# Wide products as halves outside attention, operands 64 bytes aside, and weight forms in another order

## The chip, the cores and the metric

The kernel runs on one core of a Trainium2 chip. The metric is the device time of one execution in microseconds, the median of several runs; lower is better. On the core TensorE multiplies (PE in the profile; its weight loads are PEld), VectorE (DVE) and ScalarE (ACT) work elementwise, GpSimd (POOL) and SyncE (SP) mostly issue DMAs. Each engine runs its own instructions in a fixed order and waits on semaphores for the others.

## The reference

A trunk of two decoder layers on 512 tokens of width 1024, in float32. Layer 0 mixes tokens by attention (8 forgetting heads, 8 stick-breaking heads), layer 1 by a gated short convolution. After each comes an MLP with a causal convolution of width 3 between up-projection and gate, inner width 2816. What the change touches is this (`rms_norm` and `causal_dwconv`, the sum of three shifted products, left out):

```python
def short_conv_mixer(h, norm_g, w_in, conv_w, w_out):
    xn = rms_norm(h, norm_g)
    proj = xn @ w_in
    gate_b = proj[..., :CONV_WIDTH]
    gate_c = proj[..., CONV_WIDTH:2 * CONV_WIDTH]
    u = proj[..., 2 * CONV_WIDTH:]
    y = gate_b * causal_dwconv(gate_c * u, conv_w)
    return y @ w_out

def conv_ffn(h, norm_g, w_up, conv_w, w_down):
    xn = rms_norm(h, norm_g)
    u = causal_dwconv(xn @ w_up, conv_w)
    g, val = u[..., :D_FF], u[..., D_FF:]
    return (jax.nn.silu(g) * val) @ w_down
```

The result of each mixer and of each MLP is added to the running activations.

## The kernel before

**Arithmetic.** A float32 operand is split into a high part, rounded to TensorE's reduced format (fp32r), and the low part that is left. A product is three matmuls: high by high, low by high, high by low. Of a weight block ScalarE makes the high part `whi` and VectorE, from it, the low part `wlo`. Both stand in rings of three buffers, so a form can be made only when TensorE has done with the third one before it.

**Two kinds of product.** A plain product (`mm3`) is three matmuls of 128 rows by 512 tokens. It is used in attention, in its output projection, in the first two of the eleven groups of columns of the first MLP, in the first block of the convolution's input projection and in its output projection. The others are made by a scheme of seven products for a 2 by 2 block multiplication (class `Sevens`): each group of 256 columns has seven weight forms, sums of quarter blocks X, Y, W, Z, and seven forms of the activations, named p1, p7, p3, p6, p2, q5, q4. Each of the seven is 24 matmuls of 256 tokens (line 1083). Quarter blocks come by DMAs issued by SP, and by accumulating DMAs issued by POOL. `Sevens.slot(g, s)` emits product number s of group g and behind it what later ones need: `weights_of` makes a weight form (lines 1031 and 1033), `kept` copies a bank of results (P7s and Xs) out before it is written again, `left`, `early` and `join` bring finished quarters to SBUF. In slot 4 `Xs` is copied from the bank to which q5 then adds. `table` is set for the two MLPs and not for the convolution. The convolution's forms carry a c in their names (`whi_q5c3` is form q5 of group 3); an MLP's carry layer and group (`wlo_p202` is form p2, layer 0, group 2).

**Down projections.** Line 1685, also by seven forms. In layer 0 the weights' 256 columns stream past activations as weights of the array; in layer 1 it is the other way, and 512 columns stream: 462 such matmuls. The activations' forms for it (`act`) take the places of the forms p6 and p2 of the up projection, their weights `whi` and `wlo` come by `load` (lines 317 and 318).

**Stages**, by the trace: attention to 256.7 us, its output projection's end to 273.5, plain blocks of the first MLP to 319.3, its seven-form blocks to 491, its down projection to 602, the convolution's first block to 626, its seven-form blocks to 727, its output projection to 772, the second MLP's up projection to 990, its down projection to 1103.

**What sets the order.** A scheduler takes the emitted program and orders each engine's instructions by modelled times and priorities; `pin` keeps an instruction at its place in the program, and `behind(x, y)` puts x after y. `spend(us)` tells it how much time of TensorE has passed, and `chores` (elementwise work left over, such as the convolution taps at line 449 and the scaling at lines 1343 and 1351) are worked off at a given rate. So an edit in one place can move instructions elsewhere. In the last MLP's start (L74 in the profile) the order is strictly that of the program.

## Time and profile before

| | us |
|---|---|
| median of 3 runs | 1109.64 (1108.37 to 1110.54) |
| the profiled execution | 1110.35 |
| its span, first to last instruction | 1108.2 |
| TensorE busy | 1089.2 |
| VectorE busy | 960.3 |
| ScalarE busy | 683.7 |
| POOL busy | 181.3 |

The granted clock of TensorE was 1.000 throughout. A row of the timeline has start and duration in microseconds, engine, line, operation, output and inputs, shapes, and in brackets the idle time before it and what ended it. Numbers of names are left out there. Matmuls overlap in the record: a row of 0.28 us may have its successor start 0.11 later, and it is the starts that tell the pace. A row of the waits names the engine, what waited, for what, and then the total in us, how many times, and the longest.

### The profile page before, as it was taken

How to read it: one execution, taken by the hardware profiler on the slowest of the kernel's cores; microseconds unless marked ns; L12 is line 12 of the kernel's file. 1: busy time of each engine (PE TensorE's matmuls, PEld its weight loads, DVE VectorE, ACT ScalarE, POOL GpSimd, SP SyncE). 2: the span in 40 equal slices, each digit the busy share in tenths (PEclk: the TensorE clock that was granted, in tenths of full speed). 3: DMA queues.
4: the chain of work that ended last, by engine and by line, in shares of the span. 5: the costliest groups of instructions: out<-in, count | busy, mean ns of one | idle time of the engine just before them, and what ended most of it. 6: DMA issues, size and time to landing. Idle time of an engine off the chain costs nothing.

```text
span 1108.2 us, 19897 instructions
## 1 busy us (share of the span) xinstructions
PE 1089.2 (98%) x7875; PEld 992.0 (90%) x7875; DVE 960.3 (87%) x1482; ACT 683.7 (62%) x1020; POOL 181.3 (16%) x206
## 2 busy tenths in 40 slices
PE   9999999999999999999999999999999999999998
PEld 7888787878889999999998899877999999998886
DVE  6798898997899788799979889776899999899886
ACT  7466667655567667676558655545666657567653
POOL 4011111101012221014401001011111221014300
PEclk9999999999999999999999999999999999999999
DMA  6678878688578988899955766596979887799951
GB/s 197 171 182 197 204 172 220 177 220 228 157 178 206 202 207 196 216 274 217 230 164 142 179 153 154 118 259 173 218 184 217 200 208 182 206 273 201 244 147 57
DMA packets 178109, 214.10 MB, mean 193 GB/s; under 512 B 7676, under 2 KB 143916, under 8 KB 178016
## 3 DMA queue, kind: packets, MB, share of 16 engines
q0 software_dynamic: 53280, 95.34, 44.6%
q1 hardware_dynamic: 124576, 117.42, 33.2%
q8 instruction: 62, 1.02, 0.3%
q14 instruction: 31, 0.25, 0.1%
q10 hardware_dynamic: 160, 0.07, 0.0%
HBM read 205.72 MB, written 44.04 MB: 225 GB/s over the span
## 4 chain that ended last, share of the span: by engine, by line
PE 57%; issue 14%; DVE 14%; DMA 9%; ACT 3%; POOL 1%; SPq 1%; DVEq 0%; ACTq 0%; POOLq 0%
PE psb L1685 10%; PE psb L1083 8%; PE psa L1685 7%; DMA three<-in_ffn_w_up 5%; PE psb L338 5%; PE psb L340 4%; PE psb L339 4%; PE psa L1083 3%; DVE wlo_p L1033 3%; PE psb L714 2%; DMA raw<-in_conv_w_out 2%; PE psa L811 2%; DMA Xc<-in_conv_w_in 1%; DMA raw<-in_ffn_w_down 1%; DVE wlo L318 1%
## 5 line engine op out<-in xcount | busy, mean ns | idle before, releaser
L1083 PE MATMUL psb<-p_hi,whi_p 128*128 128x256 f32 x480 | 132.9, 277 | 0.0
L1083 PE MATMUL psb<-p_hi,wlo_p 128*128 128x256 f32 x480 | 132.5, 276 | 0.1
L1083 PE MATMUL psb<-p_lo,whi_p 128*128 128x256 f32 x480 | 132.6, 276 | 0.0
L317 ACT ACTIVATE whi<-raw 128x1024 fp32r<-128x1024 f32 (+2 forms) x77 | 79.0, 1027 | 74.8 <-PE psb L339 22.0
L318 DVE TENSOR_TENSOR wlo<-raw,whi 128x1024 fp32r<-128x1024 f32 (+2 forms) x77 | 90.9, 1181 | 26.7 <-ACT whi L317 26.2
L1083 PE MATMUL psb<-q_hi,wlo_q 128*128 128x256 f32 x320 | 89.3, 280 | 2.0 <-DVE wlo_q L1033 1.9
L1083 PE MATMUL psa<-p_hi,wlo_p 128*128 128x256 f32 x320 | 89.9, 281 | 1.2 <-DVE wlo_p L1033 0.8
L1083 PEld LDWEIGHTS psb<-p_hi,wlo_p 128*128 128x128 f32 x480 | 90.0, 188 | 0.4 <-DVE wlo_p L74 0.4
L1083 PEld LDWEIGHTS psb<-p_hi,whi_p 128*128 128x128 f32 x480 | 90.1, 188 | 0.0
L1083 PEld LDWEIGHTS psb<-p_lo,whi_p 128*128 128x128 f32 x480 | 90.1, 188 | 0.0
L1083 PE MATMUL psb<-q_hi,whi_q 128*128 128x256 f32 x320 | 88.7, 277 | 0.3 <-ACT Xs L1145 0.2
L1083 PE MATMUL psa<-p_lo,whi_p 128*128 128x256 f32 x320 | 88.6, 277 | 0.0
L1083 PE MATMUL psa<-p_hi,whi_p 128*128 128x256 f32 x320 | 88.6, 277 | 0.0
L1083 PE MATMUL psb<-q_lo,whi_q 128*128 128x256 f32 x320 | 88.4, 276 | 0.0
L338 PE MATMUL psb<-hs_a,whi 128*128 128x512 f32 x176 | 72.9, 416 | 0.0
L340 PE MATMUL psb<-hs_a,wlo 128*128 128x512 f32 x176 | 69.6, 396 | 0.0
L1083 PEld LDWEIGHTS psa<-p_hi,wlo_p 128*128 128x128 f32 x320 | 60.0, 188 | 3.2 <-DVE wlo_p L1033 2.6
L1083 PEld LDWEIGHTS psb<-q_hi,wlo_q 128*128 128x128 f32 x320 | 60.0, 188 | 3.2 <-DVE wlo_q L1033 2.8
L1685 PE MATMUL psb<-act,whi 128*128 128x256 f32 x352 | 60.8, 277 | 0.9 <-DVE act L1035 0.7
L1083 PEld LDWEIGHTS psb<-q_hi,whi_q 128*128 128x128 f32 x320 | 60.1, 188 | 0.7 <-ACT Xs L1145 0.4
L1083 PEld LDWEIGHTS psa<-p_hi,whi_p 128*128 128x128 f32 x320 | 60.1, 188 | 0.3 <-ACT whi_p L1031 0.2
L1083 PEld LDWEIGHTS psa<-p_lo,whi_p 128*128 128x128 f32 x320 | 60.1, 188 | 0.0
(554 smaller groups left out, 3647.0 us busy)
## 6 DMA issues: line engine op xcount, KB each, us to landing
t<-in_ffn_w_up POOLq DMA_DIRECT2D x24, 768.0 KB, 8.2
raw<-in_attn_w_in SPq DMA_DIRECT2D x24, 512.0 KB, 5.2
t<-in_ffn_w_up POOLq DMA_DIRECT2D x12, 1024.0 KB, 10.3
X<-in_ffn_w_up SPq DMA_DIRECT2D x20, 512.0 KB, 5.0
Y<-t SPq DMA_DIRECT2D x20, 512.0 KB, 7.3
three<-t SPq DMA_DIRECT2D x20, 512.0 KB, 5.7
W<-in_ffn_w_up SPq DMA_DIRECT2D x20, 512.0 KB, 3.8
Z<-in_ffn_w_up SPq DMA_DIRECT2D x20, 512.0 KB, 5.6
```

The costliest lines, as they stand in the source:

```text
L317: return (act.activation(hi[:, at_], raw[:, at_], AF.Copy), dve.tensor_tensor(lo[:, at_], raw[:, at_], f32(hi[:, at_]), op=ALU.subtract))
L318: dve.tensor_tensor(lo[:, at_], raw[:, at_], f32(hi[:, at_]), op=ALU.subtract))
L338: made = [pe.matmul(acc, w[0], rhs[0], start=first, stop=False), pe.matmul(acc, w[0], rhs[1], start=False, stop=False), pe.matmul(acc, w[1 ...
L339: pe.matmul(acc, w[0], rhs[1], start=False, stop=False),
L340: pe.matmul(acc, w[1], rhs[0], start=False, stop=last)]
L714: pe.matmul(ss[e][:, c:c + wide], ql[rows, b * P:n], kl[rows, 0:wide], start=first and b == bs[0], stop=last and b == bs[-1])
L811: pe.matmul(out_, w, t[:, first:first + step * (NB - k - 1) + 1:step, :], start=k == 0 and i == 0, stop=k == NB - 1 and i == 1)
L1033: rest = dve.tensor_tensor(lo, src, f32(hi), op=ALU.subtract)
L1083: pe.matmul(to, w[a][:, k, c], x[b][:, k, :], start=fresh and i + k + t == 0, stop=i == 1 and k == 3 and t == 2, skip_group_check=not fresh)
L1685: pe.matmul(to, l, r, start=begin and o + t == 0, stop=end and t == 2 and o == (0 if layer else 1), skip_group_check=not fresh)
```

## The change

Three things are edited. First, from the output projection of attention on, `mm3` makes each of its three matmuls as two of 256 tokens (`pieces`): 540 of them become 1080, while 516 in attention stay. The last down projection's 462 become 924 in the same way. Each half loads its weights anew, so 1002 matmuls and 1002 weight loads are added. Second, the last down projection's operands, weights and activations, are placed 16 floats (64 bytes) further on in their tiles (`ASIDE`, `begins`, `form_tile`); the tiles of four forms grow by 128 bytes. Third, forms are made elsewhere in the program: without a table, q4's weights in slot 3 instead of 4, so ahead of the copy `Xs`, and the next group's p1 ahead of `left` in slot 5; the activations' p3 a slot later; in the second MLP p1's first weights ahead of the last but one residual; and two sums of its norm later (`EARLY`).

```diff
--- before.py
+++ after.py
@@ -34,6 +34,7 @@
...
+ASIDE = 16
...
@@ -50,7 +51,7 @@
 PLAIN = 2, 0
 FAR = 41
 CHUNKS = ((2, 3), (5, 3), (8, 3)), ((0, 3), (3, 4), (7, 4))
-EARLY, LATER = 4.0, 5.0
+EARLY, LATER = 6.0, 5.0
 SHARE = 0.58
 
 
@@ -263,7 +264,7 @@
             pass
 
 
-    wanted, ready, at, halve = [], [], [0], {}
+    wanted, ready, at, halve, begins = [], [], [0], {}, {}
 
     def want(dram, k0, nk, c0, n, *more):
         wanted.append((dram, k0, nk, (c0, n) + more))
@@ -297,6 +298,7 @@
 
         hi = wp.tile([P, CHUNK], F32R, tag="whi", name=f"whi{i}", bufs=3)
         lo = wp.tile([P, CHUNK], F32R, tag="wlo", name=f"wlo{i}", bufs=3)
+        begin_ = begins.get(i, 0)
...
@@ -313,11 +315,11 @@
                 to += width
 
         def part(a, b):
-            at_ = slice(a * n, b * n)
-            return (act.activation(hi[:, at_], raw[:, at_], AF.Copy),
-                    dve.tensor_tensor(lo[:, at_], raw[:, at_], f32(hi[:, at_]), op=ALU.subtract))
+            at_, to = slice(a * n, b * n), slice(begin_ + a * n, begin_ + b * n)
+            return (act.activation(hi[:, to], raw[:, at_], AF.Copy),
+                    dve.tensor_tensor(lo[:, to], raw[:, at_], f32(hi[:, to]), op=ALU.subtract))
         halve[i] = part, nk
-        return [t[:, 0:nk * n].rearrange("p (k c) -> p k c", c=n) for t in (hi, lo)]
+        return [t[:, begin_:begin_ + nk * n].rearrange("p (k c) -> p k c", c=n) for t in (hi, lo)]
 
     def split_all(i):
         part, nk = halve.pop(i)
@@ -333,11 +335,12 @@
         at[0] += 1
         return ready[at[0] - 1]
 
+    pieces = [(slice(0, S),)]
+
     def mm3(acc, w, rhs, first, last):
 
-        made = [pe.matmul(acc, w[0], rhs[0], start=first, stop=False),
-                pe.matmul(acc, w[0], rhs[1], start=False, stop=False),
-                pe.matmul(acc, w[1], rhs[0], start=False, stop=last)]
+        made = [pe.matmul(acc[:, c], w[x], rhs[y][:, c], start=first and x + y + c.start == 0, stop=last and x == 1 and c.stop == S)
+                for x, y in ((0, 0), (0, 1), (1, 0)) for c in pieces[0]]
         spend(0.65)
         return made
 
@@ -487,6 +490,7 @@
             want(ffn_w_up[layer], 0, 8, DFF + j * P, P)
 
     HF, HT = NF // 2, S // 2
+    LEFT, RIGHT = slice(0, HT), slice(HT, S)
...
@@ -1006,6 +1010,7 @@
         nxt.feed(o, h[:, o, :])
 
     norm = Norm("n1", 0)
+    pieces[0] = LEFT, RIGHT
     run(output_part((4,), range(2), "c"))
     run(output_part(range(4), (3,), "b"))
     fetch(AHEAD - 1)
@@ -1038,7 +1043,6 @@
                 pin(m)
         return rest
 
-    LEFT, RIGHT = slice(0, HT), slice(HT, S)
     FORMS = ("p1", "p7", "p3", "p6", "p2", "q5", "q4")
     HEAD = 7
 
@@ -1085,11 +1089,17 @@
                         stop=i == 1 and k == 3 and t == 2, skip_group_check=not fresh)
                 spend(0.35)
 
+    WIDER = [f"{n}_{i}" for n in ("p6", "p2") for i in ("hi", "lo")]
+
+    def form_tile(mp, tag, name, begin_=0):
+        t = mp.tile([P, 4 * HT + (2 * ASIDE if tag in WIDER else 0)], F32R, tag=tag, name=name)
+        return t[:, begin_:begin_ + 4 * HT].rearrange("p (k t) -> p k t", t=HT)
+
     class Sevens:
 
         def __init__(self, name, mp, groups, block_of):
             self.name, self.mp, self.groups, self.block_of = name, mp, groups, block_of
-            self.forms = {n: [mp.tile([P, 4, HT], F32R, tag=f"{n}_{i}", name=f"{n}_{i}{name}") for i in ("hi", "lo")] for n in FORMS}
+            self.forms = {n: [form_tile(mp, f"{n}_{i}", f"{n}_{i}{name}") for i in ("hi", "lo")] for n in FORMS}
             self.st, self.wides, self.table, self.scaled = {}, {}, None, False
 
         def load_pair(self, g):
@@ -1208,20 +1218,25 @@
                     self.early(p, st[p]["R"])
                 if on:
                     self.weights_of(g, "q5", "X")
+                    if not self.table:
+                        self.weights_of(g, "q4", "four")
             elif s == 4:
                 if on:
                     self.kept(g, "Xs", c["R"])
-                    self.weights_of(g, "q4", "four")
+                    if self.table:
+                        self.weights_of(g, "q4", "four")
             if was and s != 2:
                 self.tail(p, s)
             if s == 5:
                 if on:
                     self.load_one(g, "Z", self.block_of(g, 1, 1))
                     self.open_wides(g)
+                    if soon and not self.table:
+                        self.weights_of(g + 1, "p1", "X")
                     self.left(g, c["A"])
-                if soon:
+                if soon and self.table:
                     self.weights_of(g + 1, "p1", "X")
-                elif on and self.ahead:
+                elif on and self.ahead and not soon:
                     self.weights_of(g, "p3", "Z")
             elif s == 6:
                 if on:
@@ -1506,7 +1521,7 @@
                 behind(raw.make("q5"), up.summed)
             if s == 1:
                 up.weights_of(0, "p2", "W")
-            if s == 2:
+            if s == 3:
                 behind(raw.make("p3"), up.rest)
             if s == 30:
                 hold, summed = tiny.tile([P, 1], F32, tag="hold", name="hold", bufs=1), up.st[4]["X"][:, 0, 0:1]
@@ -1516,9 +1531,9 @@
                 behind(conv(7, wides[3]["yg"][:, 1, :])[0], up.joined)
                 fetch(1)
         for s in (0, 2, 3):
-            up.slot(5, s)
             if s == 0:
                 fetch(2)
+            up.slot(5, s)
         return ys, place
 
     def mlp(layer, norm, mp, begun_up=None):
@@ -1526,7 +1541,6 @@
         acts, c1, c2 = {}, {}, {}
         PHASES = ("p1", "p7", "p2", "p6", "p3", "q5", "q4")
         steps = [(p, g) for p in range(7) for g in range(len(GROUPS))]
-        act_tags = [f"{n}_{i}" for n in ("p6", "p2") for i in ("hi", "lo")]
 
         def tile_at(tag, name, bufs=1):
             return mp.tile([P, 2 * S], F32, tag=tag, name=f"{name}_{layer}", bufs=bufs)
@@ -1560,6 +1574,8 @@
                     want_sum(two(g), nk, 512, block(0 if name == "p6" else 1, 0, k0, False))
         if layer == 0:
             want_conv()
+        else:
+            begins.update((i, ASIDE) for i in range(begun, len(wanted)))
 
         SOURCE = {"p1": ("a", 1.0), "p7": ("b", 1.0), "p6": ("b", 1.0), "p2": ("d", -1.0), "q5": ("a", -1.0), "p3": ("b", -1.0), "q4": ("c", 1.0)}
 
@@ -1569,7 +1585,8 @@
             p, g = steps[i]
             k0, nk = GROUPS[g]
             name, sign = SOURCE[PHASES[p]]
-            t = acts[i] = mp.tile([P, 2, 2, HT], F32R, tag=act_tags[i % 4], name=f"act{layer}_{i}")
+            t = form_tile(mp, WIDER[i % 4], f"act{layer}_{i}", ASIDE if layer else 0).rearrange("p (x k) t -> p x k t", x=2)
+            acts[i] = t
             halves_to(t[:, 0, 0:nk, :], t[:, 1, 0:nk, :], blocks.block(name, k0, nk), sign, held=("act", "dve") if p else ())
 
         def sums(i):
@@ -1682,7 +1699,9 @@
                                 to, l, r = acc[b], acts[i][:, x, k, b * P:(b + 1) * P], w[y][:, k, :]
                             else:
                                 to, l, r = acc[b][:, o * HT:(o + 1) * HT], w[y][:, k, (2 * b + o) * P:(2 * b + o + 1) * P], acts[i][:, x, k, :]
-                            pe.matmul(to, l, r, start=begin and o + t == 0, stop=end and t == 2 and o == (0 if layer else 1), skip_group_check=not fresh)
+                            for c in (LEFT, RIGHT) if layer else (LEFT,):
+                                part = to[:, c] if layer else to
+                                pe.matmul(part, l, r[:, c], start=begin and o + t + c.start == 0, stop=end and t == 2 and o + c.start > 0, skip_group_check=not fresh)
                 spend(1.4 * nk / 2)
 
             late = len(steps) - 1 - AHEAD
@@ -1755,6 +1774,8 @@
             w, acc = weights(), bank("ab"[o % 2])
             out_products(w, acc, range(ND))
             strict[0] = o == ND - 1
+            if o == 6:
+                up.weights_of(0, "p1", "X")
             residual_out(o, acc)
             if o == 3:
                 raw.make("p1")
@@ -1764,7 +1785,6 @@
                 for n in ("p6", "p2", "q5", "q4"):
                     raw.make(n, slice(0, 2))
             elif o == 6:
-                up.weights_of(0, "p1", "X")
                 raw.make("p6", slice(2, 3))
                 up.first_sums(0)
                 for n in ("p2", "q5", "q4"):
```

POOL's and SP's instructions keep their order. On VectorE, ScalarE and TensorE some change places, also where nothing is edited. Three such places follow; line numbers of the changed kernel are a few higher (L449 is L452 there, L1033 is L1038, L1343 is L1358).

VectorE at the start of the first MLP, around the low part of form p2, group 2 (`wlo_p202`); L449 and L1343 are chores on the plain blocks. Before:

```order
L1033 TENSOR_TENSOR wlo_p602_3836<-three02_3762,whi_p602_3835 128x1024
L449 SCALAR_TENSOR_TENSOR uv00_3536<-yv00_3534,taps_117,uv00_3536 128x510
L1343 TENSOR_TENSOR hs_a_wide0_3852<-psb201_3602,nrow_n1_3526 128x512
L1070 TENSOR_TENSOR head_blocks0_3402<-ug00_3535,uv00_3536 128x256
L1071 SCALAR_TENSOR_TENSOR head_blocks0_3402<-ug00_3535,uv00_3536 128x256
L1343 TENSOR_TENSOR hs_a_wide0_3852<-psb202_3643,nrow_n1_3526 128x512
L1343 TENSOR_TENSOR hs_a_wide0_3852<-psc203_3688,nrow_n1_3526 128x512
L1343 TENSOR_TENSOR hs_a_wide0_3852<-psc204_3725,nrow_n1_3526 128x512
L449 SCALAR_TENSOR_TENSOR hs_a_wide0_3852<-hs_a_wide0_3852,taps_117 128x511
L1033 TENSOR_TENSOR wlo_p202_3844<-W02_3801,whi_p202_3843 128x1024
L1033 TENSOR_TENSOR wlo_q502_3879<-X02_3684,whi_q502_3878 128x1024
L449 SCALAR_TENSOR_TENSOR hs_a_wide0_3852<-hs_a_wide0_3852,taps_117 128x510
```

And with the change:

```order
L1038 TENSOR_TENSOR wlo_p602_4088<-three02_4014,whi_p602_4087 128x1024
L1074 TENSOR_TENSOR head_blocks0_3462<-ug00_3652,uv00_3653 128x256
L1075 SCALAR_TENSOR_TENSOR head_blocks0_3462<-ug00_3652,uv00_3653 128x256
L1358 TENSOR_TENSOR hs_a_wide0_4104<-psb202_3823,nrow_n1_3643 128x512
L1358 TENSOR_TENSOR hs_a_wide0_4104<-psc203_3892,nrow_n1_3643 128x512
L1358 TENSOR_TENSOR hs_a_wide0_4104<-psc204_3953,nrow_n1_3643 128x512
L452 SCALAR_TENSOR_TENSOR hs_a_wide0_4104<-hs_a_wide0_4104,taps_117 128x511 x2
L452 SCALAR_TENSOR_TENSOR hs_a_wide0_4104<-hs_a_wide0_4104,taps_117 128x510 x2
L1038 TENSOR_TENSOR wlo_p202_4096<-W02_4053,whi_p202_4095 128x1024
L1038 TENSOR_TENSOR wlo_q502_4131<-X02_3888,whi_q502_4130 128x1024
L1074 TENSOR_TENSOR head_blocks0_3462<-hs_a_wide0_4104 128x256
```

Four L452 on `hs_a_wide` stand ahead of `wlo_p202`, where one L449 on it stood. The one on `uv` and the first L1343 have moved ahead of `wlo_p602`, and so stand ahead of `wlo_p202` as before.

ScalarE in the convolution, from group 3's form q5 to group 4's p7; `Xsc3` is the copy that q5's product waits for, L445 a multiplication of the gate that waits for VectorE. Before:

```order
L1031 ACTIVATE whi_q5c3_8345<-Xc3_8018 128x1024
L1145 ACTIVATE Xsc3_8377<-psb257_8281 128x512
L1031 ACTIVATE whi_q4c3_8379<-Yc3_8019 128x1024
L445 ACTIVATE hs_a_conv_7720<-hs_a_conv_7720,gains_116 128x512 x2
L1134 ACTIVATE hs_a_conv_7720<-psa255_8218 128x2x256
L1031 ACTIVATE whi_p1c4_8413<-Xc4_8250 128x1024
L1031 ACTIVATE whi_p7c4_8442<-Yc4_8251 128x1024
```

And with the change:

```order
L1036 ACTIVATE whi_q5c3_8693<-Xc3_8366 128x1024
L1036 ACTIVATE whi_q4c3_8697<-Yc3_8367 128x1024
L448 ACTIVATE hs_a_conv_8068<-hs_a_conv_8068,gains_116 128x512
L1155 ACTIVATE Xsc3_8729<-psb257_8629 128x512
L448 ACTIVATE hs_a_conv_8068<-hs_a_conv_8068,gains_116 128x512
L1036 ACTIVATE whi_p1c4_8760<-Xc4_8598 128x1024
L1144 ACTIVATE hs_a_conv_8068<-psa255_8566 128x2x256
L1036 ACTIVATE whi_p7c4_8790<-Yc4_8599 128x1024
```

`Xsc3` has moved behind `whi_q4c3` and the first of the L445 (now L448), and `whi_p1c4` ahead of the copy at L1134 (now L1144).

VectorE at the start of the second MLP, around the first weight form (`wlo_p110`); L1737 adds a residual, L1313 prepares the activations' forms. Before:

```order
L1033 TENSOR_TENSOR q4_lo1_8740<-hs_a_conv_7720,q4_hi1_8739 128x512
L1033 TENSOR_TENSOR q5_lo1_8738<-s1_up_8742,q5_hi1_8737 128x512
L1737 TENSOR_TENSOR h_120<-psa267_8976,h_120 128x512
L1313 TENSOR_TENSOR s0_up_8741<-s0_up_8741,hs_a_conv_7720 128x256
L1313 TENSOR_TENSOR s1_up_8742<-hs_a_conv_7720 128x256
L384 TENSOR_TENSOR nacc_n3_8726<-nacc_n3_8726,sq_n36_9003 128x512
L1033 TENSOR_TENSOR wlo_p110_9007<-X10_8890,whi_p110_9006 128x1024
L1033 TENSOR_TENSOR p6_lo1_8734<-s0_up_8741,p6_hi1_8733 128x256
L1033 TENSOR_TENSOR wlo_p710_9014<-Y10_8891,whi_p710_9013 128x1024
```

And with the change:

```order
L1038 TENSOR_TENSOR q4_lo1_9088<-hs_a_conv_8068,q4_hi1_9087 128x512
L1038 TENSOR_TENSOR wlo_p110_9518<-X10_9334,whi_p110_9517 128x1024
L1038 TENSOR_TENSOR q5_lo1_9086<-s1_up_9090,q5_hi1_9085 128x512
L1756 TENSOR_TENSOR h_120<-psa267_9468,h_120 128x512
L1328 TENSOR_TENSOR s0_up_9089<-s0_up_9089,hs_a_conv_8068 128x256
L1328 TENSOR_TENSOR s1_up_9090<-hs_a_conv_8068 128x256
L387 TENSOR_TENSOR nacc_n3_9074<-nacc_n3_9074,sq_n36_9523 128x512
L1038 TENSOR_TENSOR p6_lo1_9082<-s0_up_9089,p6_hi1_9081 128x256
L1038 TENSOR_TENSOR p2_lo1_9084<-hs_a_conv_8068,p2_hi1_9083 128x256
L1038 TENSOR_TENSOR wlo_p710_9530<-Y10_9335,whi_p710_9529 128x1024
```

`wlo_p110` has moved up past five operations, among them the residual's addition.

## The prediction

> **What bounds the kernel now.** I read the page's engine shares first, then its chain of waits, then the timeline of TensorE, and where TensorE paused those of VectorE and ScalarE.
>
> ```profile
> span 1108.2 us, 19897 instructions
> PE 1089.2 (98%) x7875; PEld 992.0 (90%) x7875; DVE 960.3 (87%) x1482; ACT 683.7 (62%) x1020; POOL 181.3 (16%) x206
> PE 57%; issue 14%; DVE 14%; DMA 9%; ACT 3%; POOL 1%; SPq 1%; DVEq 0%; ACTq 0%; POOLq 0%
> ```
>
> TensorE is the bound, but VectorE at 87% is close behind and holds 14% of the chain. So two things can move the end: the time from one matmul's start to the next, and the short pauses in which TensorE waits for a weight form (ScalarE makes the high part `whi`, VectorE behind it the low part `wlo`). A matmul row's own duration overlaps its neighbours; the pace has to be read from starts. These are first and last rows of four stretches without a pause: plain products (129 starts on), last down projection (83), first down projection (261), attention values (22).
>
> ```profile
> 288.25 0.39 PE L339 MATMUL psa<-hs_a,whi 128*128 128x512 f32 x1
> ...
> 318.18 0.39 PE L339 MATMUL psc<-hs_b,whi 128*128 128x512 f32 x1
> ...
> 1001.95 0.39 PE L1685 MATMUL psa<-whi,act 128*128 128x512 f32 x1
> ...
> 1021.13 0.40 PE L1685 MATMUL psb<-whi,act 128*128 128x512 f32 x1
> ...
> 503.42 0.40 PE L1685 MATMUL psa<-act,whi 128*128 128x256 f32 x2
> ...
> 533.01 0.44 PE L1685 MATMUL psa<-act,whi 128*128 128x256 f32 x2
> ...
> 202.80 0.28 PE L597 MATMUL psb<-wlo,hs_a 128*128 128x256 f32 x1
> ...
> 205.39 0.28 PE L598 MATMUL psb<-whi,hs_a 128*128 128x256 f32 x1
> ```
>
> 29.93 us over 129 is 232.0 ns for a 512-wide matmul, 19.18 over 83 is 231.1 in the last down projection. A 256-wide one takes 29.59 over 261, or 113.4 ns, in the first down projection, but 2.59 over 22, or 117.7 ns, in attention. By the addresses of the compiled program the rows at 113.4 have the streamed operand 64 bytes past a multiple of 128 and the weights on one; in the attention rows it is the other way round. Whether that is what sets the 4 ns, no row shows.
>
> **The change part by part.** *Halves.* Two matmuls at 113.4 are 226.8 ns. Outside attention 540 wide products become pairs: 540 x (232.0 - 226.8) is 2.8 us gained. In the last down projection 462 do: 462 x (231.1 - 226.8) is 2.0 us. Bounds: at the attention pace a pair takes 235.4, a loss of 540 x 3.4 = 1.8 and 462 x 4.3 = 2.0 us. I take 113.4, since the first down projection is the nearest row (same line, same widths of weights) and the 64 bytes bring the last one to its placement; the other halved products have it already. Each half loads its weights again; the first down projection does so too, within its 113.4.
>
> *The start of the first MLP.* VectorE's order there changed, though no edit names it: three shift-and-add operations (L449) now come ahead of `wlo` of form p2, group 2.
>
> ```profile
> 321.11 1.22 DVE L1033 TENSOR_TENSOR wlo_p<-three,whi_p 128x1024 fp32r<-128x1024 f32 x1
> ...
> 325.97 0.75 DVE L449 SCALAR_TENSOR_TENSOR hs_a_wide<-hs_a_wide,taps 128x511 f32<-128x511 f32 x1
> 326.63 1.22 DVE L1033 TENSOR_TENSOR wlo_p<-W,whi_p 128x1024 fp32r<-128x1024 f32 x1
> 327.76 1.23 DVE L1033 TENSOR_TENSOR wlo_q<-X,whi_q 128x1024 fp32r<-128x1024 f32 x1
> ...
> 697.79 2.73 DVE L449 SCALAR_TENSOR_TENSOR hs_a_conv<-hs_a_conv,gains 128x511 f32<-128x511 f32 x4
> ...
> 327.61 0.28 PE L1083 MATMUL psa<-p_lo,whi_p 128*128 128x256 f32 x1
> 327.90 0.39 PE L1083 MATMUL psa<-p_hi,wlo_p 128*128 128x256 f32 x1
> ```
>
> Before, that form was ready at 327.85 and TensorE, at 327.61 + 0.11 = 327.72, waited 0.18. Four such operations take 2.73 us, so three add 2.0. VectorE's work there starts from the norm's row, ahead of which 117 products are halved by the order, at most 117 x 5.2 ns = 0.6 us: ready at 327.85 + 2.0 - 0.6 = 329.25. TensorE comes 252 x 5.2 ns = 1.3 us earlier, at 326.4, and waits some 2.8. Net +2.6 us. Bounds: -0.2 if VectorE gets through earlier, +2.8 if it gains nothing from the norm. Behind TensorE stand only its own next products; later forms gain, since the three operations are out of the way. One later pause can take some of it back, that of q4 in group 4, in which ScalarE waited for a DMA:
>
> ```profile
> ACT whi_q L1031 <- DMA three<-in_ffn_w_up: 4.3, 3, 2.4
> ...
> PE psb L1083 <- DVE wlo_q L1033: 0.4, 1, 0.4
> ```
>
> I give it 0.6 us back (the 0.4 and the weight load before it), between 0 (the transfer moves with TensorE) and 1.3.
>
> *The convolution.* q4's form now comes ahead of the copy `Xs`, and the next group's p1 ahead of the copy at its side. What pauses were, and what stood by:
>
> ```profile
> 636.48 0.28 PE L1083 MATMUL psa<-p_hic,wlo_p2c 128*128 128x256 f32 x1
> ...
> 637.87 0.38 PE L1083 MATMUL psb<-q_hic,wlo_q5c 128*128 128x256 f32 x1 [0.46 <-DVE wlo_q5c L1033]
> ...
> 695.27 0.28 PE L1083 MATMUL psb<-q_hic,whi_q5c 128*128 128x256 f32 x1
> ...
> 700.88 0.28 PE L1083 MATMUL psb<-q_hic,wlo_q4c 128*128 128x256 f32 x1
> ...
> 703.49 0.39 PE L1083 MATMUL psa<-p_hic,wlo_p1c 128*128 128x256 f32 x1 [0.76 <-DVE wlo_p1c L1033]
> ...
> 716.99 0.28 PE L1083 MATMUL psb<-q_hic,whi_q5c 128*128 128x256 f32 x1
> ...
> 719.60 0.28 PE L1083 MATMUL psb<-q_hic,wlo_q5c 128*128 128x256 f32 x1
> ...
> 721.67 0.39 PE L1083 MATMUL psb<-q_hic,wlo_q4c 128*128 128x256 f32 x1 [1.25 <-DVE wlo_q4c L1033]
> ...
> PE psb L340 <- DVE wlo L318: 0.3, 1, 0.3
> ```
>
> Three starts at 113.4 take 0.34 us. So 637.87 - 636.48 - 0.34 = 1.05 us went at q5 of group 0, 2.27 at p1 of group 4, 1.73 at its q4, 0.3 at the out projection's first `wlo`: 5.35 in all. The edits put each of those forms earlier. But q5's product may not start before `Xs` has been copied out of its bank, and in groups 3 and 4 `Xs` now stands behind a multiplication (L445) that waits for VectorE:
>
> ```profile
> 694.25 0.58 ACT L1145 ACTIVATE Xsc<-psb 128x512 f32<-128x512 f32 x1
> ...
> 696.77 0.73 ACT L445 ACTIVATE hs_a_conv<-hs_a_conv,gains 128x512 f32<-128x512 f32 x1 [1.00 <-DVE hs_a_conv L1452]
> ...
> 718.19 0.72 ACT L445 ACTIVATE hs_a_conv<-hs_a_conv,gains 128x512 f32<-128x512 f32 x1 [1.95 <-DVE hs_a_conv L1452]
> ```
>
> In group 3 `Xs` then ends at 696.77 + 0.73 + 0.58, less 0.1 by which neighbouring rows overlap, 697.98; q5 starts 2.71 later than at 695.27, and p1's third matmul comes 50 starts on at 703.65, against 703.49: the 2.27 is spent. In group 4 `Xs` ends at 719.39, q4's third matmul 26 starts on at 722.34, against 721.67: +0.67. Sum: -1.05 + 0.16 + 0.67 - 0.3 = -0.5 us. Bounds: -5.35 if `Xs` does not hold q5, +0.5 if group 0's pause stays.
>
> *The start of the second MLP.* Its first `wlo` is made earlier and its norm's row later:
>
> ```profile
> 772.21 0.28 PE L1083 MATMUL psa<-p_lo,whi_p 128*128 128x256 f32 x1
> 773.25 0.38 PE L1083 MATMUL psa<-p_hi,wlo_p 128*128 128x256 f32 x1 [0.76 <-DVE wlo_p L1033]
> ...
> PE psc L412 <- DVE nacc_n L74: 0.8, 1, 0.8
> ...
> 787.31 0.36 PE L1083 MATMUL psb<-q_hi,wlo_q 128*128 128x256 f32 x1
> ...
> 785.94 1.23 DVE L74 TENSOR_TENSOR wlo_q<-X,whi_q 128x1024 fp32r<-128x1024 f32 x1
> ...
> 792.30 1.23 DVE L74 TENSOR_TENSOR p_lo<-s_up,p_hi 128x1024 fp32r<-128x1024 f32 x1 [1.13 <-ACT p_hi L74]
> 793.44 0.69 DVE L74 TENSOR_TENSOR y_both<-psb,P7s 128x512 f32<-128x512 f32 x1
> ```
>
> Two pauses go (0.93 and 0.8). VectorE's work up to q5's `wlo`, though, is the same set in another order, and that form ended at 787.1, just ahead of the matmul at 787.31: of the 1.7 us some 0.4 stays. Further on two more operations like the last row now precede the second group's p7 form. The gap of 1.13 would hold them, but the first needs a product that ends only about then, so I count +0.5. Together +0.1, bounds -2.0 and +1.0.
>
> *Sum:* -2.8 - 2.0 + 2.6 - 0.6 - 0.5 + 0.1 = -3.2 us. The profiled execution took 1110.35 us, 2.2 more than its span, and lies 0.7 above the median; by it 1107.2, from the median of 1109.64 **1106.5 us**, which I name.
>
> **The rivals.** *All of it pays:* `Xs` does not hold q5, and the second MLP's pauses go: -4.8 + 2.0 (start of the first MLP) - 5.35 - 2.0 = -10.1, or 1099.5. For it: in groups 0 and 1 no L445 stands before `Xs`. Against: the wait just worked out.
>
> *Halves hidden:* only the last down projection, where nothing but TensorE runs at the end, shows its gain; elsewhere forms made by VectorE at 87% set the time. -2.0 + 2.6 - 0.6 + 0.5 = +0.5: 1110.1.
>
> *Slower, each matmul costs something of its own:* 1002 pairs at 2 x 117.7 = 235.4 ns, with the other terms as forecast: +1.8 + 2.0 + 2.6 - 0.6 - 0.5 + 0.1 = +5.4, or 1115.0. It decides from the point where a pair costs more than 232. For it: the attention rows. Against: 261 starts at 113.4 on the very line.
> By the Trainium skill, "TensorE: Matmul & The Clock Gate", section "Back-to-back issue gap", an isolated warm matmul takes its columns divided by 2.4 plus 2.5 ns; by that a pair costs 2.5 ns more than a wide one, an estimate of 2.5 us lost where I have 4.8 gained, and 1113.8 us. The trace does not agree: its pair of 226.8 stands under its wide one of 232.
>
> *The 64 bytes do nothing:* the last down projection's halves run at 117.7, a loss of 2.0 instead of a gain: 1110.5.
> The Trainium skill, "SBUF — State Buffer", section "Who interferes with whom", says that TensorE never waits on anyone at its memory; by it the placement should change nothing. The two paces of 256-wide rows neither prove nor refute this.
>
> **How the numbers follow.** Forecast 0.47, all pays 0.15, halves hidden 0.22, slower 0.08, 64 bytes 0.08. The forecast's own range is 1104 to 1108.5. About 0.2% (2.2 us) can be told from no change, so faster means under 1107.4. Faster: nine tenths of the forecast, all of the first rival, a tenth of the second: 0.59. Slower, over 1111.9: the slow rival and a little of the two near 1110: 0.10. The rest, 0.31, is no change. The range 1101 to 1111 leaves out the far part of the first rival and the slow one, about 0.2.
>
> **What will show it.** Starts 113 to 114 ns apart at the halved lines, both in the plain products and in the last down projection; 117 or more there is the slow rival or the last. A wait of 2 to 3 us before p2's third matmul in group 2 of the first MLP, with `wlo` behind four L449 rows. In the convolution, a q5 of groups 3 and 4 whose first matmul waits for `Xs` (2 us or more) and no pause at p1 of group 4. At the second MLP no pause at its first `wlo` and the third matmul of q5 0.4 us sooner after the end of the out projection than before. I am wrong in the sum if VectorE passes L445's source earlier than before (then `Xs` is not late), or if later pauses of the first MLP grow with the delay instead of taking it up.

## The result: slower, and the profile after

The changed kernel took 1112.36 us (median of 20 runs, 1109.26 to 1119.38), the kernel before, in as many runs beside it, 1108.70 (1105.96 to 1111.45). The ratio is 1.0035, with a 95% interval of 1.0023 to 1.0047: by it the change is some 3.9 us slower. The forecast was 1106.5, with 1101 to 1111.

The head of the page of the changed kernel:

```profile
span 1110.1 us, 21903 instructions
PE 1094.5 (99%) x8877; PEld 1046.3 (94%) x8877; DVE 960.8 (87%) x1482; ACT 688.6 (62%) x1020; POOL 182.9 (16%) x206
PE 71%; DVE 15%; issue 8%; DMA 4%; ACT 2%; POOL 0%; DVEq 0%; ACTq 0%; POOLq 0%
```

TensorE is busy 5.3 us longer than before, and idle 15.6 us where it was 19.0. The pauses did get fewer; the matmuls themselves take more. The first starts of six products in a row show where (p3, p6, p2, q5, q4 and the next p1 in the first MLP, 24 matmuls each). Timeline of TensorE, kernel before:

```profile
341.50 0.28 PE L1083 MATMUL psb<-p_hi,whi_p 128*128 128x256 f32 x1
...
344.22 0.28 PE L1083 MATMUL psb<-p_hi,whi_p 128*128 128x256 f32 x1
...
346.94 0.28 PE L1083 MATMUL psa<-p_hi,whi_p 128*128 128x256 f32 x1
...
349.66 0.28 PE L1083 MATMUL psb<-q_hi,whi_q 128*128 128x256 f32 x1
...
352.38 0.28 PE L1083 MATMUL psb<-q_hi,whi_q 128*128 128x256 f32 x1
...
355.10 0.28 PE L1083 MATMUL psa<-p_hi,whi_p 128*128 128x256 f32 x1
```

And the same six in the changed kernel:

```profile
343.23 0.28 PE L1087 MATMUL psb<-p_hi,whi_p 128*128 128x256 f32 x1
...
345.95 0.28 PE L1087 MATMUL psb<-p_hi,whi_p 128*128 128x256 f32 x1
...
348.77 0.28 PE L1087 MATMUL psa<-p_hi,whi_p 128*128 128x256 f32 x1
...
351.65 0.28 PE L1087 MATMUL psb<-q_hi,whi_q 128*128 128x256 f32 x1
...
354.51 0.28 PE L1087 MATMUL psb<-q_hi,whi_q 128*128 128x256 f32 x1
...
357.36 0.28 PE L1087 MATMUL psa<-p_hi,whi_p 128*128 128x256 f32 x1
```

Before, every product takes 2.72 us, 24 x 113.4 ns. After, p3 does too, but p6 takes 2.82, p2 2.88, q5 2.86 and q4 2.85, some 117 to 120 ns a matmul, without a wait among them. Over all 25 groups of the changed kernel's trace p6 and p2 run so every time (means of 117.4 to 120.1 ns), q5 and q4 in nine groups each, about every third, and of p1, p7 and p3 one product in 75; before, 9 of all 175 products were over 116. These products were not edited. What changed for them is where their operands lie: by the addresses of the compiled program the tiles of p6 and p2 have grown by 128 bytes, so that the low part of each starts 4224 bytes behind the high one instead of 4096, and all that lies behind is moved.

The halves, in the changed kernel: first and last row of a stretch of the convolution's output projection (378 starts), of the first down projection (482) and of the last (254).

```profile
729.96 0.39 PE L342 MATMUL psa<-y,wlo 128*128 128x256 f32 x2
...
772.80 0.39 PE L342 MATMUL psb<-y_hi,wlo 128*128 128x256 f32 x2
...
503.89 0.28 PE L1704 MATMUL psa<-act,whi 128*128 128x256 f32 x1
...
560.00 0.28 PE L1704 MATMUL psa<-act,wlo 128*128 128x256 f32 x1
...
1050.04 0.40 PE L1704 MATMUL psb<-wlo,act 128*128 128x256 f32 x2
...
1079.97 0.64 PE L1704 MATMUL psb<-whi,act 128*128 128x256 f32 x4
```

The plain halves run at 42.84 over 378, 113.3 ns, as forecast. The first down projection, not edited either, has gone from 113.4 to 116.4. (In it the activations' 256 tokens stream past the weights, and in the last one the weights stream past the activations; the text on the kernel before has the first the other way round.) The last one's halves take 29.93 over 254, 117.8 ns: a pair 235.6, more than the wide matmul's 231.1.

The two waits that the prediction had put into numbers, at p2 of group 2 in the first MLP and at q5 of group 3 in the convolution:

```profile
326.88 0.28 PE L1087 MATMUL psb<-p_hi,wlo_p 128*128 128x256 f32 x1
328.09 0.39 PE L1087 MATMUL psa<-p_hi,whi_p 128*128 128x256 f32 x1 [0.93 <-ACT whi_p L1036]
...
329.65 0.38 PE L1087 MATMUL psa<-p_hi,wlo_p 128*128 128x256 f32 x1 [1.05 <-DVE wlo_p L1038]
...
325.74 2.72 DVE L452 SCALAR_TENSOR_TENSOR hs_a_wide<-hs_a_wide,taps 128x511 f32<-128x511 f32 x4
328.37 1.22 DVE L1038 TENSOR_TENSOR wlo_p<-W,whi_p 128x1024 fp32r<-128x1024 f32 x1
...
697.57 0.28 PE L1087 MATMUL psa<-p_hic,wlo_p2c 128*128 128x256 f32 x1
700.14 0.38 PE L1087 MATMUL psb<-q_hic,whi_q5c 128*128 128x256 f32 x1 [2.29 <-ACT Xsc L1155]
...
698.88 0.72 ACT L448 ACTIVATE hs_a_conv<-hs_a_conv,gains 128x512 f32<-128x512 f32 x1 [1.48 <-DVE hs_a_conv L1467]
699.51 0.58 ACT L1155 ACTIVATE Xsc<-psb 128x512 f32<-128x512 f32 x1
```

Both are there. Before p2's third matmul TensorE lost 329.65 - 326.88 - 0.34 = 2.4 us (0.2 before the change), part of it to `whi`, which stands behind three multiplications that ScalarE now makes first. q5 of group 3 starts 2.5 us late, behind `Xs` and the multiplication L448. In group 4, for which the prediction had a wait of the same kind, no pause is over 0.2 us.

The wait for `Xs` has a sequel that no term of the prediction holds. From 701.1 to 704.5 us the granted clock of TensorE was 0.50, and q5's matmuls ran at half their pace:

```profile
702.96 0.41 PE L1087 MATMUL psb<-q_loc,whi_q5c 128*128 128x256 f32 x1
...
704.45 0.32 PE L1087 MATMUL psb<-q_hic,wlo_q5c 128*128 128x256 f32 x1
704.61 0.28 PE L1087 MATMUL psb<-q_hic,whi_q4c 128*128 128x256 f32 x1
...
706.15 0.28 PE L1087 MATMUL psb<-q_loc,whi_q4c 128*128 128x256 f32 x1
```

Seven starts of q5 take 1.49 us, 213 ns each; the 13 of q4 behind them take 1.54, 118 each. Fifteen matmuls of q5 ran so, which cost an estimated 1.5 us (15 x 100 ns). In the trace of the kernel before the clock was 1.00 until the last matmul.

### The profile page after: what moved, and what is told of

Read it like the earlier page. It is cut to its first block, busy times and chain, and to the rows that moved or that the text cites. A ratio compares the mean times of both kernels' runs of the same rounds, so it can differ in the third digit from the quotient of the medians.

```text
span 1110.1 us, 21903 instructions
## 1 busy us (share of the span) xinstructions
PE 1094.5 (99%) x8877; PEld 1046.3 (94%) x8877; DVE 960.8 (87%) x1482; ACT 688.6 (62%) x1020; POOL 182.9 (16%) x206
## 4 chain that ended last, share of the span: by engine, by line
PE 71%; DVE 15%; issue 8%; DMA 4%; ACT 2%; POOL 0%; DVEq 0%; ACTq 0%; POOLq 0%
PE psb L1087 18%; PE psb L342 13%; PE psb L1704 11%; PE psa L1704 8%; PE psa L1087 7%; PE psa L342 3%; DMA three<-in_ffn_w_up 3%; DVE wlo_p L1038 3%; PE psb L718 2%; PE psa L815 2%; DVE wlo L320 1%; PE psc L790 1%; PE psb L600 1%; PE psb L601 1%; PE psb L602 1%
## 5 line engine op out<-in xcount | busy, mean ns | idle before, releaser
L342 PE MATMUL psb<-hs_a,whi 128*128 128x256 f32 (+1 forms) x360 | 93.9, 343 | 0.0
L342 PE MATMUL psb<-hs_a,wlo 128*128 128x256 f32 (+1 forms) x240 | 69.5, 333 | 0.0
L342 PEld LDWEIGHTS psb<-hs_a,whi 128*128 128x128 f32 x360 | 57.1, 188 | 8.4 <-issue 3.2
```

What stands on the lines that cost most here:

```text
L342: made = [pe.matmul(acc[:, c], w[x], rhs[y][:, c], start=first and x + y + c.start == 0, stop=last and x == 1 and c.stop == S) for x, y in ...
```

## The experiments

All times are medians, and each ratio is to the kernel before, run on the same chip in the same series. The ratio is formed over the runs of the series and need not be the quotient of two medians. "Products" are the seven-form products and the last column the halves or wide matmuls of the last down projection, both as mean start-to-start times of the trace over all matmuls without a pause.

| kernel | us | ratio, 95% | products ns | last down ns |
|---|---|---|---|---|
| before | 1108.70 | 1 | 113.7 | 231.2 wide |
| the change | 1112.36 | 1.0035 (1.0023-1.0047) | 115.4 | 117.8 |
| e1 all but the 64 bytes | 1111.06 | 1.0000 (0.9985-1.0014) | 113.6 | 117.8 |
| e2 before, tiles 128 wider | 1112.85 | 1.0013 (0.9998-1.0029) | 115.7 | 231.4 wide |
| e3 the change, tiles 256 wider | 1110.92 | 1.0006 (0.9993-1.0020) | 113.8 | 117.8 |
| e4 order alone | 1106.69 | 0.9966 (0.9953-0.9980) | 113.8 | 231.2 wide |
| e12 order, tiles 128 wider | 1111.33 | 1.0006 (0.9990-1.0022) | 115.7 | 231.3 wide |
| e8 order, second MLP | 1111.46 | 1.0007 (0.9992-1.0023) | 114.0 | 231.1 wide |
| e14 order, convolution | 1107.37 | 0.9980 (0.9963-0.9996) | 113.8 | 231.2 wide |
| e15 plain halves alone | 1110.54 | 0.9999 (0.9980-1.0019) | 113.9 | 231.3 wide |
| e6 order, plain halves | 1109.73 | 0.9987 (0.9974-0.9999) | 113.7 | 231.1 wide |
| e13 order, late plain halves | 1108.14 | 0.9974 (0.9961-0.9988) | 113.8 | 231.3 wide |
| e5 order, down halves, low parts 128 aside | 1108.62 | 0.9985 (0.9971-0.9999) | 113.7 | 116.7 |
| e7 as e5, late plain halves | 1108.44 | 0.9977 (0.9967-0.9988) | 113.6 | 116.8 |
| e9 order, down halves aligned | 1107.51 | 0.9977 (0.9959-0.9996) | 114.1 | 117.5 |
| e10 order, gap | 1107.73 | 0.9968 (0.9951-0.9986) | 114.2 | 230.2 wide |
| e11 as e9, late plain halves | 1109.98 | 0.9986 (0.9970-1.0002) | 114.1 | 117.6 |

The kernel before had medians of 1110.4 to 1111.4 in the four series of the experiments, so ratios are compared and not times.

### Is it the place of the tiles? (e1, e2, e3, e12)

The theory after the first look was that the wider tiles slow unedited products; the rival, that more matmuls or weight loads do, or a lower clock. In e1, e2, e3 no engine's order differs from that of the kernel each was made from; only addresses do.

In e1, against the change:

```diff
-ASIDE = 16
+ASIDE = 0
```

In e2, against the kernel before (and so for the `act` tiles):

```diff
+    def form_tile(mp, tag, name):
+        t = mp.tile([P, 4 * HT + (32 if tag in WIDER else 0)], F32R, tag=tag, name=name)
+        return t[:, 0:4 * HT].rearrange("p (k t) -> p k t", t=HT)
...
-            self.forms = {n: [mp.tile([P, 4, HT], F32R, tag=f"{n}_{i}", name=f"{n}_{i}{name}") for i in ("hi", "lo")] for n in FORMS}
+            self.forms = {n: [form_tile(mp, f"{n}_{i}", f"{n}_{i}{name}") for i in ("hi", "lo")] for n in FORMS}
```

In e3, against the change:

```diff
-        t = mp.tile([P, 4 * HT + (2 * ASIDE if tag in WIDER else 0)], F32R, tag=tag, name=name)
+        t = mp.tile([P, 4 * HT + (64 if tag in WIDER else 0)], F32R, tag=tag, name=name)
```

> The changed kernel with the 64 bytes taken back (ASIDE = 0), so that the tiles of forms p6 and p2 keep their old size and every tile behind them its old place; halves and order stay, and no engine's order differs. Theory (the wider tiles moved the forms' addresses, and with them the seven-form products slowed from 113.7 to 115.4 ns and the first down projection from 113.5 to 116.5): both go back, 4200 x 1.7 + 924 x 3 = about 10 us less than the changed kernel, 1101 to 1104 us. The last down projection's halves, with streamed operands on a multiple of 128 bytes, 117 to 118 ns. Rival (the halves themselves slow everything, by their weight loads or by the clock): the seven-form products stay at 115 and the time within 2 us of the changed kernel's.

> The kernel before with nothing but the tiles of forms p6 and p2 made 128 bytes wider, as the change has them; no halves, no other order. Theory (addresses): the seven-form products at 115 to 116 ns instead of 113.7, the first down projection at 116 to 117, and the kernel 8 to 10 us slower than before. Rival (halves or clock): the time of before within 2 us.

> The changed kernel, its p6 and p2 tiles 256 bytes wider instead of 128, the operands of the last down projection 64 bytes in as in the change. All forms then start at 64 past a multiple of 256. Theory in its narrow form (a form's high and low tiles must start alike modulo 256): the seven-form products back at 113.5 to 114 and the time at 1102 to 1105 us. If the old places themselves matter (all forms 576 past a multiple of 1024 there): q5, q4 and the forms between stay at 115 or more and the time near 1110. Rival (halves or clock): no difference from the changed kernel.

By the products' pace the theory held in all three: p6 and p2 are slow in all 25 groups of e2, and in at most one of e1 and of e3. The same six products in e2 (the kernel before with nothing but wider tiles), and four of them in e3:

```profile
341.45 0.28 PE L1083 MATMUL psb<-p_hi,whi_p 128*128 128x256 f32 x1
...
344.18 0.28 PE L1083 MATMUL psb<-p_hi,whi_p 128*128 128x256 f32 x1
...
347.00 0.28 PE L1083 MATMUL psa<-p_hi,whi_p 128*128 128x256 f32 x1
...
349.88 0.28 PE L1083 MATMUL psb<-q_hi,whi_q 128*128 128x256 f32 x1
...
352.73 0.28 PE L1083 MATMUL psb<-q_hi,whi_q 128*128 128x256 f32 x1
...
355.58 0.28 PE L1083 MATMUL psa<-p_hi,whi_p 128*128 128x256 f32 x1
```

```profile
345.99 0.28 PE L1087 MATMUL psb<-p_hi,whi_p 128*128 128x256 f32 x1
...
348.71 0.28 PE L1087 MATMUL psa<-p_hi,whi_p 128*128 128x256 f32 x1
...
351.43 0.28 PE L1087 MATMUL psb<-q_hi,whi_q 128*128 128x256 f32 x1
...
354.15 0.28 PE L1087 MATMUL psb<-q_hi,whi_q 128*128 128x256 f32 x1
```

With 128 bytes more, p6 to q4 take 2.82 to 2.88 us; with 256 more, 2.72 again. So it is neither the halves nor the size but the place. By the addresses of the compiled programs every form starts 64 bytes past a multiple of 256 when the tiles are 256 wider; when they are 128 wider, the high parts of p6 and p2 do and their low parts start 192 past one.

By the time the theory fell short. It had given 10 us (4200 x 1.7 ns + 924 x 3); e1 won back 0.35%, some 3.9 us, e3 0.29%, and e2 lost only 0.13%, an interval that just reaches 1. The heads of the pages of e1 and e2 hint why:

```profile
span 1109.3 us, 21903 instructions
PE 1090.4 (98%) x8877; PEld 1040.2 (94%) x8877; DVE 959.8 (87%) x1482; ACT 685.0 (62%) x1020; POOL 182.8 (16%) x206
```

```profile
span 1109.4 us, 19897 instructions
PE 1096.3 (99%) x7875; PEld 1002.7 (90%) x7875; DVE 960.3 (87%) x1482; ACT 685.6 (62%) x1020; POOL 181.5 (16%) x206
```

In e2 TensorE is busy 7.1 us longer than before, but idle only 13.1 us against 19.0. In e1 it is busy 4.1 us less than in the changed kernel and idle 3.3 longer. Some of these differences are the clock's: matmuls at 213 ns, behind long waits, are 40 in e1's trace, 14 in e2's and 15 in the changed kernel's, so that without them e1 would be busy an estimated 2.5 us less still (25 x 100 ns). A large part of the matmuls' time seems to be exchanged for waits, since forms that come late by VectorE and the DMAs come at the same time either way; that reason is argued from these sums and not tested by itself.

e12 has the same line with 32 in place of 64, on the kernel with the order edits alone (e4, below):

> The order edits with p6's and p2's tiles 128 bytes wider, no halves. Theory (the wider tiles keep p6 and p2 in TensorE's slower rhythm of 117 to 118 ns, and q5 and q4 behind them): seven-form products at 115.4 instead of 113.5 ns in the trace, and 3 to 6 us slower than the order edits alone (0.9966 of before), so 0.999 to 1.003. Rival (the products' lost time is taken out of waits, as 20 us of waits fell to 13 on the kernel before): 0.996 to 0.998.

With the order edits in, the wider tiles cost the difference of 0.9966 and 1.0006, some 4.4 us, as the theory said. They cost about as much on top of all edits (1.0000 and 1.0035). A lower clock is not the cause: the mean granted clock of e1's runs, 0.9970, is not above the changed kernel's 0.9975, and e12's 0.9973 is near e4's 0.9976.

### The order edits (e4, e8, e14)

e4 is the change without its halves and its 64 bytes:

```diff
-ASIDE = 16
+ASIDE = 0
...
-    pieces[0] = LEFT, RIGHT
...
-                            for c in (LEFT, RIGHT) if layer else (LEFT,):
+                            for c in (slice(0, S),) if layer else (LEFT,):
```

e8 takes from it what concerns the convolution (q4's and p1's forms at their old places in `slot`, the activations' p3 a slot earlier, the fetch after the last group's slot); e14 keeps that and takes the rest:

```diff
-EARLY, LATER = 6.0, 5.0
+EARLY, LATER = 4.0, 5.0
...
-            if o == 6:
-                up.weights_of(0, "p1", "X")
             residual_out(o, acc)
...
             elif o == 6:
+                up.weights_of(0, "p1", "X")
```

> Only the order edits (q4's and p1's forms earlier, p3 and the norm's sums later); no halves, no wider tiles, nothing 64 bytes aside. Theory: pauses of TensorE fall as in the changed kernel's trace, from 20 to 15 us in all with q5 of group 3 waiting some 2.5 us: 2 to 4 us faster than before. Rival (the order is what costs the time): 3 us or more slower than before.

> The order edits of the second MLP's start alone (p1's first forms earlier, the norm's sums later); the convolution's forms as before, no halves, nothing aside. Theory (in the convolution the pauses taken away come back as q5's wait for Xs, so its edits are worth nothing, and what the order gains lies at the second MLP): 0.995 to 0.998 of before. Rival (the gain is the convolution's): 0.999 to 1.001.

> The order edits of the convolution alone; the second MLP's start as before. Theory (q5's wait for Xs eats what the earlier forms gain): 0.999 to 1.001 of before. Rival (the gain of the order edits, 0.9966, is the convolution's, as the second MLP's edits alone gave 1.0007): 0.996 to 0.998.

The order alone is 3.8 us faster, the lowest ratio of all kernels, though several lie within its interval. The convolution's part gives 0.9980 and so about 2.2 of them (by the medians 4.0), the second MLP's part alone nothing that can be told from zero. Here theory lost to its rival: I had held the convolution's edits worthless, because in the trace q5 of group 3 waits for `Xs`.

That wait is in e14's trace too (start-to-start 4.78 us), and there the convolution's output projection starts 2 us late. But that trace is of an execution 2.4 us over the median (1109.76), and e4's of the slowest of its twelve (1109.67). In both the granted clock was 0.50 for 6.8 us behind the wait, and 20 or so matmuls ran at 213 ns. e5 (below) has the same order edits, and its trace shows the wait (3.35 us from start to start) with the clock at 1.00 throughout: there the time from the first product of group 0 to the first of the second MLP is 2.7 us shorter than before, since the pauses of groups 0 and 4 are gone and group 3 loses 1.4. So in that execution, whose clock stays up, the forms made earlier gain what e14's ratio says.

That the executions differ by the clock fits e14's runs: the fastest (1105.64) is the only one at 1.000. Of the 13 traces with the convolution's order edits, 12 have such a stretch of 3.4 or 6.8 us behind the wait; of the four without, e2's alone has one before the last matmul, at 707 us behind two pauses of 1 us. No run tests whether the wait is its cause.

What the two parts do together beyond their sum (about 2.4 us by the ratios) is of the size of the intervals.

### The plain halves (e6, e13, e15)

e15 is the kernel before with the new `mm3` and the line that sets `pieces`. e6 is e4 with that line; in e13 it stands further down:

```diff
+        pieces[0] = LEFT, RIGHT
         ys, place = conv_seven(norm, mp, rp)
```

> The kernel before with nothing but its plain products as halves. Theory (they gain 2.5 us at 113.7 ns, but the scheduler, which counts time by what TensorE has been given, puts three more shift-and-add operations ahead of p2 of group 2, with a wait of 2 to 4 us there): 0.999 to 1.002 of before, with that wait in the trace. Rival (the wait comes from the edits of the order): no wait there and 0.997 to 0.998.

> The order edits and the plain products as halves; the last down projection whole, nothing aside. Theory (the plain halves run at 113.7 and gain 2.5 us, but with them the scheduler puts three more shift-and-add operations ahead of form p2 of group 2 and TensorE waits 2 to 3 us there): no better than the order edits alone, 0.996 to 0.999 of before. Rival (more matmuls cost time of their own or lower the clock): 1.000 or more, as the kernel with both sorts of halves had, with products near 115 ns.

> The order edits and the plain products as halves from the convolution on; nothing else. Theory (288 products gain 4.6 ns each and nothing is put ahead of p2 of group 2 in the first MLP): 1 us under the order edits alone, 0.994 to 0.997 of before. Rival (each halved stage gives its gain back as a wait for VectorE): 0.997 to 0.999.

The halves run at 113.6 to 113.8 ns wherever they stand, so 2.5 us are gained by TensorE. e15's trace has the wait in the first MLP, although nothing but the halves was edited:

```profile
326.62 0.28 PE L1085 MATMUL psb<-p_hi,wlo_p 128*128 128x256 f32 x1
327.91 0.39 PE L1085 MATMUL psa<-p_hi,whi_p 128*128 128x256 f32 x1 [1.02 <-ACT whi_p L1033]
...
329.47 0.39 PE L1085 MATMUL psa<-p_hi,wlo_p 128*128 128x256 f32 x1 [1.05 <-DVE wlo_p L1035]
```

It is the scheduler that moves the shift-and-add operations, once its matmuls are others. e15 comes out at no change, e6 2.3 us over the order alone. About 1 us of the latter may be the clock's, an estimate from the mean of the runs (0.9967 in e6, 0.9976 in e4, the difference times 1110 us); e6's trace has half clock behind the wait at p2 too, e15's has not. In e13, where no such wait arises, the late halves still add 0.9 us to the order alone instead of taking 1.3 off, within the two intervals. The traces of e13 and e4 do not show where the gain of TensorE goes: e4's has 6.8 us at half clock in the convolution and e13's 3.4, so their later stages can't be set side by side. So plain halves gain on TensorE and not in time.

### The halves of the last down projection (e5, e7, e9, e10, e11)

What held them at 117.8? The prediction's reason, 64 bytes, was in place. From e3 came another: like starts of high and low parts modulo 256. Their streamed operands, the weights' high and low parts, lie in rings of 4224-byte buffers and never start alike. e5, with the order edits and nothing 64 bytes aside, moves the low part by 128 bytes:

```diff
+        low = 32 if i in begins else 0
...
+            to_low = slice(low + a * n, low + b * n)
...
-                    dve.tensor_tensor(lo[:, to], raw[:, at_], f32(hi[:, to]), op=ALU.subtract))
+                    dve.tensor_tensor(lo[:, to_low], raw[:, at_], f32(hi[:, to]), op=ALU.subtract))
```

e9 has the 64 bytes, the tiles 256 bytes wider as in e3, whole plain products, and a gap of 128 bytes between the rings; e10 is e4 with the gap alone:

```diff
+        if i == 0:
+            wp.tile([P, 32], F32, tag="gap", name="gap", bufs=1)
         lo = wp.tile([P, CHUNK], F32R, tag="wlo", name=f"wlo{i}", bufs=3)
```

> The order edits and the last down projection as halves, nothing 64 bytes aside; instead the low parts of its weights (the streamed operand there) begin 128 bytes further into their tile, so that the high and the low part of a block start alike modulo 256 bytes, at 0 or 128. Theory (matmuls that stream high and low parts in turn keep 113.4 ns when both start alike modulo 256, and take 117 to 118 when they don't; the 64 bytes have no part in it): its halves at 113 to 114 ns, a pair 4.4 ns under a wide matmul's 231.2, and 2 us faster than the order edits alone (0.9966 of before), so 0.993 to 0.997. Rival (it is the 64 bytes modulo 128 that count, and something else spoiled them): halves at 117 to 118 and 2 us slower than the order edits alone.

> The order edits and the last down projection as halves with its operands 64 bytes aside, and now a gap of 128 bytes between the buffers of the high and of the low weights, so that a block's high and low part start alike modulo 256; the tiles of p6 and p2 are 256 bytes wider, so the forms start alike too. Theory (113.4 ns needs both: the streamed operand 64 past a multiple of 128 with the weights on one, and high and low alike modulo 256): the halves of the last down projection at 113 to 114 ns, 116.65 without the 64 bytes and 117.8 without the like start. A pair then gains 4.4 ns on 231.2, 2 us in all. Rival (something else in that stage holds them, the way its weights alternate): 116 to 118 as before. The attention values, whose streamed weights now start alike at 0 or 128, tell the like start alone: 117.6 before, 116.5 to 117 by the theory.

> The order edits and the gap of 128 bytes between high and low weights, with no halves and nothing 64 bytes aside. Theory: matmuls of 512 columns do not care (231 to 232 ns as before, in the last down projection too, where high and low now start alike), the seven-form products stay at 113.4 to 114, and the time is that of the order edits alone, 0.995 to 0.998 of before. Rival (wide matmuls too run faster when the parts start alike): the last down projection's at 227 to 229 ns and 1 to 2 us less.

Neither theory held. e5 gives 116.7 on average, e9, which has both, 117.5; e5's rival had named 117 to 118 and a loss of 2 us against the order alone, and by the ratios it is 2.1. The attention values, which e9 was to tell apart, went from 117.5 to 117.0 ns with like starts, as expected there. In e9's trace, 256 starts apart:

```profile
1049.88 0.63 PE L1705 MATMUL psb<-whi,act 128*128 128x256 f32 x4
...
1080.03 0.40 PE L1705 MATMUL psb<-wlo,act 128*128 128x256 f32 x2
```

That is 117.8 ns. e5's mean hides something else, which four rows 24 starts apart show:

```profile
1085.11 0.51 PE L1705 MATMUL psb<-whi,act 128*128 128x256 f32 x3
...
1087.92 0.51 PE L1705 MATMUL psb<-whi,act 128*128 128x256 f32 x3
...
1090.66 0.50 PE L1705 MATMUL psb<-whi,act 128*128 128x256 f32 x3
...
1093.38 0.51 PE L1705 MATMUL psb<-whi,act 128*128 128x256 f32 x3
```

2.81, 2.74 and 2.72 us: there are two rhythms, 113.4 and 117 to 118 ns, and no values between that last. The same pair of buffers ran in the fast one at 993 and at 1015 us of e5's trace and in the slow one at 1049. So place alone does not set the rhythm in this stage; what a stretch begins with seems to count too. What does set it is open.

> As the kernel with the low parts 128 bytes aside, and the plain products as halves from the convolution on only, so that nothing before it is ordered otherwise. Theory: 288 plain products gain 4.6 ns each, 1.3 us, on top of that kernel, unless VectorE holds the start of the second MLP: 0.992 to 0.997 of before. Rival (each halved product costs something of its own): slower than that kernel by 1 us or more.

> The kernel with aligned halves in the last down projection, and the plain products from the convolution on as halves as well. Theory: aligned halves gain 2 us and the late plain halves 1.3 on the order edits alone, 0.992 to 0.996 of before. Rival (fewer nanoseconds a matmul come back as waits for VectorE and the DMAs, since these set the stages): no faster than the order edits alone, 0.996 to 0.999.

e7 and e11 are e5 and e9 with e13's line. Neither beats the order alone, and both miss what the theory gave; e11 came out as its rival had it. e11 held a hint for the like starts: its plain halves slowed to 116.5 ns on average, and there the gap had put the high and low parts of the convolution's result on unlike places, 64 and 192 modulo 256. In the changed kernel and in e7 and e13 (113.7 to 113.8) they start alike. e10's wide matmuls gained 1 ns, its time nothing.

No kernel tried has a lower ratio than the order alone. 462 pairs of halves at 117.5 cost about 2 us by the trace over wide matmuls; in time, all edits but the 64 bytes (e1) are 1.4 us over e6, which has no halves in that stage.

## Why the prediction was wrong

**The step that failed first** is one that the prediction left out: that the tiles of p6 and p2 grow by 128 bytes was costed at nothing, not even as a term with bounds. It moves operands of four of the seven products and of the first down projection, and these went from 113.4 ns to between 116.4 and 120, the products p6 and p2 in every group and q5 and q4 in about every third. Shown: 0.35% between the change and e1, 0.40% between e4 and e12, both with the order unchanged. I had read the addresses of the rows at 113.4 and 117.7, and had asked what 64 bytes would do for the last down projection, but not what the room for them does to everything behind it.

**The halves of the last down projection**, -2.0 us: the mechanism was wrong, not the size only. They run at 117.8, the upper bound that the prediction gave, +2.0 by the trace. That the 64 bytes bring them to 113.4 was an inference from two groups of rows that differed in many things. The rival "the 64 bytes do nothing" was right about this stage: the halves took 117.8 with them (the change) and without (e1).

**The plain halves**, -2.8 us: right on TensorE (113.3 ns, 2.5 us), wrong that they would show in time. For this term "halves hidden" was the better rival, though by another way: e15 gives 0.9999, and its trace has the wait at p2 that the halves bring about.

**The start of the first MLP**, +2.6 us: right, a pause of 2.4 against 0.2. I named its cause on VectorE; ScalarE's three multiplications took part. The 0.6 that was to come back later did not in e15's trace, where nothing but the plain halves was edited: it is 1.5 us behind the kernel before at the first product of group 3 and 2.3 at the first of the convolution.

**The convolution**, -0.5 us: the wait for `Xs` in group 3 came as worked out (2.5 us; forecast 2.7), the pause at p1 of group 4 went. But the sum was mis-sized. The 0.67 us that group 4 was to lose did not come, since `Xs` held nothing up there and the pause at q4 is gone. And the stretch at half clock behind the wait, an estimated 1.5 us in this trace, was put at nothing. The edits alone give some 2.2 us (e14), and 2.7 in the trace without such a stretch (e5).

**The start of the second MLP**, +0.1: e8 agrees with about nothing. In the changed kernel's trace the first group takes 1.5 us less than before and the second 2.2 more. The wait at the second group's p7 is larger than the +0.5 I counted:

```profile
796.45 0.27 PE L1623 MATMUL psc<-ident,h 128*128 128x128 f32 x1
797.91 0.38 PE L1087 MATMUL psb<-p_hi,wlo_p 128*128 128x256 f32 x1 [1.18 <-DVE wlo_p L75]
```

**The slow rival**, that each matmul costs something of its own, gave a time on the right side for a reason that the runs refute: 378 plain halves at 113.3 ns, and the products back at 113.6 on average with all the extra matmuls present (e1). The same rows stand against the rule cited with it, from the Trainium skill, "TensorE: Matmul & The Clock Gate", section "Back-to-back issue gap", by which a pair would cost 2.5 ns more than a wide matmul: two halves took 226.6 and a wide one 232. The statement cited from the Trainium skill, "SBUF — State Buffer", section "Who interferes with whom", that TensorE never waits on anyone at its memory, does not foresee e2: with nothing but other addresses the four products from p6 to q4 of the group shown took 11.40 us instead of 10.88.

So, step by step from the kernel before to the changed one, by the ratios: order -3.8 us (e4), plain halves +2.3 (e6 over e4), halves of the last down projection +1.4 (e1 over e6), the 64 bytes with their wider tiles +3.9 (the change over e1). Each step has an interval of some 2 us. The forecast had -0.4 for the order, -0.8 for the plain halves with the wait they bring, -2.0 for the other halves and nothing for the tiles: all but the first were too low by 3 us or more, and the order's gain, larger than forecast, hid a part of that.
